# Pages for weights at sixteen 4-byte places of a 64-byte line, in a seven-product fp32r matmul kernel

## The chip, the cores and the metric

The kernel runs on one NeuronCore of a Trainium2 chip, as one launch. The metric is the device time of that launch in microseconds, lower is better. Times are medians over runs; the profile is one execution taken apart by the hardware profiler.

## The reference

The depth is one, so only the short-convolution layer of the model runs, on 1024 positions of width 1024 with an inner width of 2048. All data is float32.

```python
D_MODEL = 1024; SEQ = 1024; D_INNER = 2048; SC_WIDTH = 3; EPS = 1e-6

def rms_norm(x, g):
    return x * rsqrt(mean(x * x, axis=-1) + EPS) * g

def short_conv_mixer(u, w_in, conv_w, w_out):
    z, bg, cg, v = split(u @ w_in, 4, axis=-1)      # w_in: 1024 x 8192
    y = bg * causal_dwconv(cg * v, conv_w) * silu(z) # 3 taps
    return y @ w_out                                 # w_out: 2048 x 1024

u = rms_norm(x, pre_norm)
out = x + rms_norm(short_conv_mixer(u, w_in, conv_w, w_out), post_norm)
```

## The kernel before

Both matrix products are done by a seven-product scheme (products `a` to `g` in place of eight half-size ones), and three of the seven (`b`, `f`, `g`) are cut by seven once more in most chunks; the pieces of that second level carry a prime (`a'` to `g'`) and the word "deep" in their tiles' names. float32 accuracy comes from splitting each operand into a high and a low part in fp32r, so one product of 128 rows costs three matmuls: low by high, high by low, high by high.

The first product takes the input's columns in 16 chunks of 128, two pairs of blocks a chunk (`p` is the pair). The moving operand of its matmuls is a U tile: the normed, transposed input, or a sum of its quarters, split into high and low. The U tiles of the first level (`u_a` to `u_g`) have a pool of their own (`up`, seven tiles of 16 KB a partition) and are read 512 columns at a time (256 for the deep products that use a half of them); the U tiles of the second level (`ubch_deep` and the like) lie in a later pool (`tmp`) and are read 256 columns at a time. The stationary operand is a block of weights, 128 by 128, out of a *page*.

A page is a tile of 512 fp32 numbers (2048 bytes) in each of 128 partitions, made by `page()`. There are 32 of them (`PAGES`). Raw weights arrive in pages from memory (`fetch`, tiles `raw`), GpSimd and VectorE form their sums in pages (`add_s`, `deep_sums`: `se`, `sc`, `sf`, `dsb`, ...), ScalarE rounds a page to its high part and VectorE subtracts that from the source to give the low part (`split`, `split_low`, `split_by_bank`: `wah` and `wal`, `dwb0h` and `dwb0l`, ...), again in pages. Snapshots of finished products (`sna`, `snc`, `sne`), y in transit, raw data of the second matrix product and the residual rows are in pages too. In the second matrix product (from about 615 us) both matmul operands lie in `up` tiles.

The whole program is recorded first and then ordered by a planner (`Plan.arrange`), which simulates the five engines with costs and due times, gives each new page a slot number (0 to 31) from a queue of free ones, and writes the order out; the pages of the head get theirs from `HEAD_SLOTS`. Engines then run their queues in that order and wait for each other by semaphores. Slot `n` is a tile with the tag `pg{n}` and one buffer; its place in SBUF follows from the order in which the tags are first asked for. In the program as built the 32 pages stand back to back from byte 117824 of a partition, 2048 bytes apart, so that each begins at a multiple of 64 bytes; the U tiles of `up` do too (bytes 3136, 19520, ...). The U tiles of `tmp` begin 32 bytes past such a multiple (191584, 193632, ...), because `gpad`, which stands ahead of them in the pool, takes 4128 bytes. The tile class below is what hands out the place.

Of the kernel before, what the change touches and what calls it, by code (L numbers as in the profile page):

```python
# [157 lines left out]
        return out  # L158


class Tile(View):

    __slots__ = ("pool", "args", "kw", "made", "parts", "writes", "reads", "left", "space", "key", "read", "summed", "n", "slot")
# [11 lines left out]
    def get(self):  # L175
        if self.made is None:
            kw = self.kw
            if kw["tag"] == "pg":
                kw = dict(kw, tag=f"pg{self.slot}", bufs=1)
            self.made = self.pool.pool.tile(list(self.args[0]), self.args[1], **kw)  # L180
        return self.made


# [1882 lines left out]
```

## Time and profile before

| what | value |
|---|---|
| time, median of 3 runs | 773.36 us (773.21 to 773.51) |
| time of the profiled execution | 772.83 us |
| its span, first to last instruction | 771.0 us |
| granted TensorE clock, mean | 0.998 |
| PE busy | 762.2 us, 4320 matmuls |
| DVE, ACT, POOL busy | 673.9, 458.8, 462.2 us |
| hardware DMA queue of SyncE | 49.0% of 16 DMA engines' span |

The profiled execution is 0.5 us below the median, and its span 1.8 us below its own time. Every compute instruction is recorded under line 252, the helper that plays a recorded operation, so instructions are told apart by their tiles' names. A matmul's duration includes its latency and overlaps that of its neighbours; how fast the matmuls follow each other is read from their starts, or from how long a run of them takes in the chain of waits.

### The profile page before, as it was taken

The page shows a single profiled execution, that of the slowest core. Times are in us where ns is not written, and L with a number is a line of the kernel's source. Part 1 is how long each engine was busy: PE and PEld are TensorE (multiplying, and loading weights), DVE is VectorE, ACT ScalarE, POOL GpSimd, SP SyncE. Part 2 cuts the span into 40 slices and gives each one's busy share as a digit, 9 for nine tenths or more (in the row PEclk, how much of TensorE's full clock was granted, in tenths as well). Part 3 has the DMA queues.
Part 4 walks back from the last instruction along what each step waited for, and adds up shares of the span by engine and source line. Part 5 has one row for each costly group of instructions (what it writes and reads, how often), then busy time and mean ns, then how long its engine had stood idle before and what let it go on. Part 6 is the DMA issues. An engine that isn't in the chain of part 4 may idle for free.

```text
span 771.0 us, 12816 instructions
## 1 busy us (share of the span) xinstructions
PE 762.2 (99%) x4320; PEld 669.6 (87%) x4320; DVE 673.9 (87%) x1022; ACT 458.8 (60%) x880; POOL 462.2 (60%) x416
## 2 busy tenths in 40 slices
PE   8999999999999999999999999999999999999996
PEld 7888889898889898888888898988888889889885
DVE  6899988989988978989999989798999898877993
ACT  7765678575656565556556565556653656564831
POOL 2519997889575778696789777584739100600321
PEclk9999999999999999999999999999999999999999
DMA  9222325243333547576858474927465998666842
GB/s 318 66 56 82 119 85 152 101 126 131 97 116 96 171 111 209 126 191 158 239 137 254 116 215 107 249 84 213 122 180 174 335 367 293 197 218 206 274 150 109
DMA packets 117137, 130.11 MB, mean 169 GB/s; under 512 B 7320, under 2 KB 74704, under 8 KB 116944
## 3 DMA queue, kind: packets, MB, share of 16 engines
q1 hardware_dynamic: 112560, 120.77, 49.0%
q0 software_dynamic: 4352, 8.39, 7.1%
q8 instruction: 34, 0.56, 0.3%
q14 instruction: 31, 0.25, 0.1%
q10 hardware_dynamic: 160, 0.14, 0.0%
HBM read 101.74 MB, written 44.30 MB: 189 GB/s over the span
## 4 chain that ended last, share of the span: by engine, by line
PE 98%; DVE 1%; DMA 0%; ACT 0%; POOL 0%; issue 0%; POOLq 0%; ACTq 0%
PE px L252 39%; PE pv L252 15%; PE po_x L252 11%; PE px2b L252 5%; PE px2f L252 4%; PE px2g L252 3%; PE po_v L252 3%; PE pp L252 3%; PE pv2b L252 3%; PE pv2f L252 2%; PE pf_x L252 1%; PE pb_x L252 1%; PE py2b L252 1%; PE pv2g L252 1%; PE py L252 1%; PE pf_v L252 1%
## 5 line engine op out<-in xcount | busy, mean ns | idle before, releaser
L252 PE MATMUL px<-u_d,wdh 128*128 128x512 f32 x248 | 76.8, 390 | 0.0
L252 PE MATMUL px<-u_a,wah 128*128 128x512 f32 x248 | 76.7, 390 | 0.0
L252 PE MATMUL pv<-u_e,weh 128*128 128x512 f32 x248 | 76.7, 390 | 0.0
L252 PE MATMUL px<-u_c,wch 128*128 128x512 f32 x248 | 76.6, 390 | 0.0
L252 ACT COPY beside<-raw 128x512 f32<-128x512 f32 x67 | 39.6, 591 | 31.8 <-DVE wal L252 11.0
L252 PEld LDWEIGHTS px<-u_d,wdh 128*128 128x128 f32 x248 | 46.6, 188 | 9.1
L252 PEld LDWEIGHTS px<-u_c,wch 128*128 128x128 f32 x248 | 46.7, 188 | 9.0
L252 PEld LDWEIGHTS px<-u_a,wah 128*128 128x128 f32 x248 | 46.7, 188 | 8.9
L252 PEld LDWEIGHTS pv<-u_e,weh 128*128 128x128 f32 x248 | 46.6, 188 | 8.9
L252 DVE SCALAR_TENSOR_TENSOR cv<-gpad,cw,cv 128x1024 f32<-128x1024 f32 x32 | 49.7, 1554 | 3.4 <-ACT cv L252 3.3
L252 POOL TENSOR_TENSOR sf<-raw,sc 128x512 f32<-128x512 f32 x30 | 44.5, 1482 | 10.9 <-DVE sc L252 6.0
L252 PE MATMUL px<-u_d,wdl 128*128 128x512 f32 x124 | 48.7, 393 | 0.0
L252 PE MATMUL px<-u_a,wal 128*128 128x512 f32 x124 | 48.7, 393 | 0.0
L252 PE MATMUL px<-u_c,wcl 128*128 128x512 f32 x124 | 48.5, 392 | 0.0
L252 PE MATMUL pv<-u_e,wel 128*128 128x512 f32 x124 | 48.5, 391 | 0.0
L252 POOL TENSOR_TENSOR sc<-se,raw 128x512 f32<-128x512 f32 x25 | 36.5, 1460 | 19.0 <-DVE se L252 10.0
L252 ACT COPY sna<-px 128x512 f32<-128x512 f32 x30 | 17.6, 586 | 49.4 <-PE px L252 47.7
L252 POOL TENSOR_TENSOR raw<-raw,raw 128x512 f32<-128x512 f32 x31 | 44.8, 1446 | 3.3 <-DVE se L252 1.9
L252 POOL TENSOR_TENSOR rs_post<-ve_post,minus_half 128x1 f32<-128x1 f32 x7 | 5.4, 784 | 68.1 <-DVE ve_post L252 68.1
L252 POOL TENSOR_TENSOR se<-raw,raw 128x512 f32<-128x512 f32 x22 | 33.1, 1504 | 17.7 <-DMA raw<-in_sc_w_in 5.7
L252 DVE TENSOR_TENSOR wcl<-sc,wch 128x512 fp32r<-128x512 f32 x31 | 31.6, 1020 | 2.6 <-ACT wch L252 2.6
L252 DVE TENSOR_TENSOR sna<-px2b,sna 128x256 f32<-128x256 f32 x56 | 23.2, 413 | 11.9 <-PE px2b L252 11.9
(486 smaller groups left out, 2637.1 us busy)
## 6 DMA issues: line engine op xcount, KB each, us to landing
raw<-in_sc_w_in SPq DMA_DIRECT2D x128, 256.0 KB, 4.6
y_d<-cv SPq DMA_DIRECT2D x16, 512.0 KB, 3.1
s_d<-s SPq DMA_DIRECT2D x32, 256.0 KB, 4.8
t_d<-in_sc_w_out POOLq DMA_DIRECT2D x16, 512.0 KB, 8.2
tb<-in_sc_w_out SPq DMA_DIRECT2D x16, 256.0 KB, 3.0
t_d<-in_sc_w_out SPq DMA_DIRECT2D x16, 256.0 KB, 4.5
t_d<-t_d SPq DMA_DIRECT2D x16, 256.0 KB, 4.5
s<-y_d SPq DMA_DIRECT2D x16, 256.0 KB, 4.7
```

The source lines that it names most:

```text
L252: getattr(engine, name)(*(self.plain(a) for a in args), **{k: self.plain(a) for k, a in kw.items()})
```

## The change

A page of a slot below 28 (`SHIFTED`) is made 8 numbers (32 bytes) longer, and the kernel uses 512 of its 520 numbers, beginning `slot // 2 % 8` numbers in. As the pages stand back to back in descending slots for the most part, their beginnings alternate between a multiple of 64 bytes and 32 past it, and the added 0 to 28 bytes give sixteen places, 4 bytes apart. Slots 28 to 31 stay as they were, and so does a shifted slot whose place comes out at 0. Everything that uses a page (DMA, the three vector engines, the weight loads) finds it at its new place. The U tiles of `up` stay at their bytes; those of `tmp` move up by 896 bytes as a whole and still begin 32 past a multiple of 64. Apart from line numbers, each engine's queue has the same instructions in the same order, on the same tiles and slots.

In the program as built, 3402 matmuls take their weights from a page. Counted by the distance in bytes, modulo 64, between the beginning of the moving operand and that of the weights:

| distance | matmuls before | matmuls after |
|---|---|---|
| 0 | 2700 | 622 |
| 32 | 702 | 280 |
| any of the other fourteen | 0 | 2500 |

Of the 3402, 2710 have their weights at a place other than a multiple of 64 bytes after the change, and none has before.

```diff
+SHIFTED = 28
+
+
 class Tile(View):
...
             kw = self.kw
             if kw["tag"] == "pg":
                 kw = dict(kw, tag=f"pg{self.slot}", bufs=1)
-            self.made = self.pool.pool.tile(list(self.args[0]), self.args[1], **kw)
+            shape = list(self.args[0])
+            whole = int(np.prod(shape[1:]))
+            at, more = 0, 0
+            if kw["tag"][:2] == "pg" and self.slot < SHIFTED:
+                at, more = self.slot // 2 % 8, 8
+            if more:
+                t = self.pool.pool.tile([shape[0], whole + more], self.args[1], **kw)[:, at : at + whole]
+                names = "abcd"[: len(shape) - 1]
+                sizes = dict(zip(names[1:], shape[2:]))
+                self.made = t.rearrange(f"p ({' '.join(names)}) -> p {' '.join(names)}", **sizes)
+            else:
+                self.made = self.pool.pool.tile(shape, self.args[1], **kw)
         return self.made
```

## The prediction

> **What bounds the kernel now.** I read the page first, then the waits of PE, then the chain of waits, stage by stage.
>
> ```profile
> span 771.0 us, 12816 instructions
> PE   8999999999999999999999999999999999999996
> PE 98%; DVE 1%; DMA 0%; ACT 0%; POOL 0%; issue 0%; POOLq 0%; ACTq 0%
> ```
>
> PE is busy in every slice, and the chain that ended last is PE for 98% of the span. The waits of PE (engine, what waited, for whom; us in total, times, longest) are these three, and asked from 60 us on, the same view has none:
>
> ```profile
> PE pw L252 <- DVE idle L252: 1.1, 1, 1.1
> PE pp L252 <- ACT u_a L252: 0.5, 1, 0.5
> PE pk L252 <- DVE xa L252: 0.3, 1, 0.3
> ```
>
> So the time is the sum of the spacings between matmuls. Only two things can move it: the spacing, or a wait that is not there now. The spacing stands in the chain of waits (start us, us, what), first in the second matrix product, where nothing alternates:
>
> ```profile
> 615.09 21.76 PE po_x L252 x96
> 636.85 2.87 PE pb_x L252 x24
> 639.73 2.88 PE pb_y L252 x24
> ```
>
> 96 matmuls of 512 columns take 21.76 us, 226.7 ns each; 24 of 256 columns take 2.88 us, 120.0 ns. Twice 120.0 less 226.7 is 13.3 ns: each matmul pays about 13.3 ns beside its columns (106.7 ns for 256), whatever their number. Times some 4200 matmuls that is 56 us, so a few ns of it are worth a few us. Now a stretch of the first product, and the weight loads of its three kinds of matmul:
>
> ```profile
> 385.89 0.70 PE px2b L252 x6
> 386.59 0.70 PE pv L252 x6
> 387.29 0.72 PE px L252 x6
> ```
>
> ```profile
> L252 PEld LDWEIGHTS px2b<-ubgh_deep,dwb 128*128 128x128 f32 x56 | 9.5, 188 | 0.5
> L252 PEld LDWEIGHTS py2b<-u_b,dwb0h 128*128 128x128 f32 x56 | 8.7, 192 | 0.0
> ```
>
> All eighteen are 256 columns by weights from a page. The first twelve read their moving operand from `ubg*_deep` and `ufg*_deep`, 32 bytes past a multiple of 64, and take 1.40 us, 116.7 ns each; the last six read `u_g`, at a multiple of 64 like the weights, and take 120.0 ns. The loads beside them last 188 ns in the first kind and 192 in the second. This is the one thing in the profile that goes with the place in a line: with weights and moving operand 32 bytes apart a matmul costs 3.3 ns less, and its load 4 ns less, than with both at the same place. When the two are read is in the timeline (start us, us):
>
> ```profile
> 419.42 0.28 PE L252 MATMUL px2f<-ufdh_deep,dwf2h 128*128 128x256 f32 x1
> 419.43 0.19 PEld L252 LDWEIGHTS px2f<-ufdh_deep,dwf2l 128*128 128x128 f32 x1
> ```
>
> The next load starts 0.01 us after a matmul does, so both begin to read at nearly the same moment. Two streams that start together at the same place of a line and meet there would explain both rows.
>
> **The change part by part.** *Spacing.* No instruction is added, removed or moved; what changes is the distance between the streams. The program has 2700 matmuls at distance 0 now and 622 after, so 2078 more are apart. If apart saves 3.3 ns wherever the two places lie (the row shows 32 bytes alone), that is 2078 x 3.3 ns = 6.9 us less. If the saving grows with the distance up to 32 bytes and falls again, the sixteen places give a part: counting each matmul of the built program by its distance (0 to 8 steps of 4 bytes, 0.41 ns a step) gives a total of 12174 steps after against 5616 before, 2.7 us less. If it grows over the whole line, to 15 steps, 7.8 us. Since a collision of two streams is there or not, I take 6.9. That a 512-column matmul saves as much is not shown; its fixed 13.3 ns being the same is why I assume it.
>
> *VectorE.* Its operands from two pages now differ in place. Neighbouring rows: the taps of the convolution read `gpad` 4 or 8 bytes past a line's beginning and `cv` 32 past it; the last row has both sources at multiples of 64.
>
> ```profile
> L252 DVE SCALAR_TENSOR_TENSOR cv<-gpad,cw,cv x32: 1268/1334/2317, 67.8 to 612.0; 128x1024 f32<-128x1024 f32 x32
> L252 DVE SCALAR_TENSOR_TENSOR u_e<-xb 128x1024 fp32r<-128x1024 f32 x2 | 2.4, 1214 | 0.0
> L252 DVE TENSOR_TENSOR gpad<-px,sna x15: 674/691/693, 83.4 to 606.4; 128x512 f32<-128x512 f32 x15
> L252 DVE TENSOR_TENSOR sne<-px,sne x31: 674/677/692, 53.6 to 609.0; 128x512 f32<-128x512 f32 x31
> ```
>
> The shortest tap (min/median/max ns) is 1268 against 1214 ns, 54 more in 1024 columns, 27 for a page. The other pair writes at 8 bytes past a line and at a line, both from 674 ns: writing off the line costs nothing. So 0 to 27 ns for an instruction with both sources in pages. In the stage with the weights (stretch; then busy us and instructions of each engine)
>
> ```profile
> 60.00:615.00 555.00, 555.00 (x3219) 490.84 (x3218) 496.97 (x739) 334.09 (x645) 411.58 (x367) 1.00 0.54 154
> ```
>
> VectorE has 739 instructions and is busy 496.97 of 555 us. At 27 ns for every one it would be 20 us more, 517 of 555: still under PE, but it delivers some low parts late:
>
> ```profile
> 419.01 0.68 DVE L252 TENSOR_TENSOR wdl<-beside,wdh 128x512 fp32r<-128x512 f32 x1
> 419.78 0.19 PEld L252 LDWEIGHTS px<-u_d,wdl 128*128 128x128 f32 x1
> ```
>
> Here `wdl` is done at 419.69 and loaded at 419.78, with 0.09 us to spare; of 587 first uses of split tiles in the trace, seven have under 0.52 us. Ten instructions in a row at 27 ns are 0.27 us late, so these few cost at most 0.3 us each, 2 us in all; and since PE itself would come sooner, the margins shrink further. I take 1.5 us, between 0 and 3. ScalarE (334 us) and GpSimd (412 us) are further from PE; the same 4% on them is hidden behind PE's 555.
>
> *DMA.* Pages are written and read by DMA off the line.
>
> ```profile
> raw<-in_sc_w_in SPq DMA_DIRECT2D x128, 256.0 KB, 4.6
> ```
>
> A raw block lands 4.6 us after its issue. No row shows a load to such a place; bounds are 0 and, at twice the time, 4.6 us later. The planner asks for pages up to 24 us ahead (`ahead`, `sync`), and no wait of PE names a DMA, so I take nothing; without that cover a late block stops GpSimd's sums, then PE.
>
> *Sum.* 772.83 (profiled) - 6.9 + 1.5 = 767.4; from the median of 773.36 it is **768.0 us**.
>
> **The rivals.** *Slower: weights off the line load longer, and the load is in the path.* For it: the 13.3 ns that do not depend on the columns look like a load that PE cannot hide. A block's 512 bytes a partition are eight lines of 64, 1.67 ns each if the 13.3 ns are their reading. Off the line they touch nine: 1.67 ns x 2710 matmuls = 4.5 us more; read as four parts of 128 bytes, each part touches three lines in place of two, half as much again, 6.7 ns x 2710 = 18 us. Against it: the deep moving operands start off a 64-byte line and got no dearer; but 32 is a round place, and 2, 4 or 12 bytes past one are not in the profile. It decides as soon as an off-line load costs more than the 6.9 us gained, 2.5 ns a matmul. At the lower price and without a gain: 773.4 + 4.5 + 1.5 = 779.4 us; at the upper, 792.9. [...]
>
> *No effect on PE: the weights' place does not matter, only the moving operand's.* The 3.3 ns would then belong to where the deep U tiles begin, which stays. For it: in the rows above the two always change together. What is left is VectorE's price: 773.4 + 0 to 1.5, say 774.0 us. [...]
>
> *A smaller gain*, by the rule that grows with the distance: 773.4 - 2.7 + 1.0 = 771.7 us, and VectorE, nearer to its bound, may eat it.
>
> **How the numbers follow.** About 0.2%, 1.5 us, is what a measurement of this kernel can tell from no change. The forecast, PE saving 5 to 9 us: 0.35. The smaller gain: 0.13, of which 0.02 ends within 1.5 us. No effect on PE: 0.18, of which 0.11 within and 0.07 slower by VectorE's late parts. Off-line loads dearer: 0.34, a third of it partly repaid by the gain but slower still. That makes faster 0.46, within 0.13, slower 0.41. Both signs hold much; the forecast's own range is 764 to 771. The whole range reaches down to 759 (the full 7.8 us, no late parts, and as much again for 512-column runs that follow 256-column ones) and up to 784, into the dearer loads, leaving out about 2 in 10, mostly the upper price.
>
> **What would show it.** In the chain of waits after the change, runs of matmuls on `u_g` or `u_b` by pages should take 116 to 118 ns each (0.70 us for six) and those of 512 columns about 223 ns, while `po_x` and `pb_x`, whose operands have not moved, stay at 226.7 and 120.0. The LDWEIGHTS of `py2b<-u_b,dwb0h` should last 188 ns, not 192. If that group or the spacing grows, it is the first rival; if both stay to the ns, the second. A wait of PE for DVE in the stage from 60 to 615 us would be VectorE's price; one for a `raw` DMA would be the cover that I counted on and did not have. The forecast is wrong if the spacing of `u_g` runs stays at 120 or above.

## The result, and the profile after

The changed kernel takes 779.70 us (median of three, 779.45 to 780.08) against 773.36: a ratio of 1.0083, 95% interval 1.0060 to 1.0105. It is 6.3 us slower; forecast was 5.4 us faster. The profiled execution took 780.08 us. The page of the changed kernel begins like that of before, PE being the chain for 98% again:

```profile
span 778.3 us, 12816 instructions
PE   8999999999999999999999999999999999999996
PE 98%; DMA 1%; ACT 0%; DVE 0%; POOL 0%; issue 0%; SPq 0%; POOLq 0%; ACTq 0%
```

Its waits of PE are all in the first stage; asked from 60 us on, the view has none:

```profile
PE pk L266 <- DVE ve_pre L266: 1.3, 1, 1.3
PE pw L266 <- DVE idle L266: 1.1, 1, 1.1
PE pk L266 <- DVE xa L266: 0.7, 1, 0.7
PE pp L266 <- ACT u_a L266: 0.5, 1, 0.5
```

The one wait that before did not have (`ve_pre`, 1.3 us) comes and goes between kernels: 0.3 us in a kernel below that took 779.58 us, none in the one that took 770.25. The stretch of the first 300 matmuls took 1.2 us longer, its waits included, so waits don't explain 6 us. The spacing does. In the stage from 60 to 615 us PE never stops, and the row of that stretch (busy us and instructions of PE, its loads, VectorE, ScalarE, GpSimd) counts what it gets through:

```profile
60.00:615.00 555.00, 555.00 (x3190) 485.58 (x3189) 476.03 (x732) 329.16 (x637) 384.12 (x365) 1.00 0.53 149
```

Before it was 3219 matmuls in the same 555 us, now 3190: 29 fewer at 172 ns is 5.0 us lost in this stage. The granted clock is 1.00 in both. The second product, whose operands have not moved, is unchanged to the hundredth in the chain of waits:

```profile
622.35 21.76 PE po_x L266 x96
644.11 2.87 PE pb_x L266 x24
646.98 2.88 PE pb_y L266 x24
```

Which matmuls got slower is in the groups by form (busy us, mean ns of one). A matmul's duration is longer than the spacing (390 ns for 512 columns that start 228.57 ns apart in the mean, before), so only its change counts. Three groups of before, and the same after:

```profile
L252 PE MATMUL px<-u_d,wdh 128*128 128x512 f32 x248 | 76.8, 390 | 0.0
L252 PE MATMUL px2b<-ubgh_deep,dwb 128*128 128x256 f32 x56 | 12.1, 279 | 0.0
L252 PE MATMUL pv2b<-u_b,dwb1h 128*128 128x256 f32 x56 | 10.7, 283 | 0.0
```

```profile
L266 PE MATMUL px<-u_d,wdh 128*128 128x512 f32 x248 | 77.7, 394 | 0.0
L266 PE MATMUL px2b<-ubgh_deep,dwb 128*128 128x256 f32 x56 | 12.2, 281 | 0.0
L266 PE MATMUL pv2b<-u_b,dwb1h 128*128 128x256 f32 x56 | 10.6, 281 | 0.0
```

512 columns cost 4 ns more, deep ones 2 ns more, and only the third kind, 256 columns from a U tile of the first level, 2 ns less. Averaging the times between neighbouring starts in the two traces (without the first 300 matmuls and without gaps above 300 ns) gives the account; "512 columns" are all matmuls of that size on `u_a` to `u_g`, "deep" those on the U tiles of the second level:

| matmuls by weights in pages | counted | before, ns | after, ns | change |
|---|---|---|---|---|
| 512 columns | 1566 | 228.57 | 232.53 | +6.2 us |
| 256 columns, `u_b`, `u_f`, `u_g` | 936 | 119.37 | 118.53 | -0.8 us |
| 256 columns, deep | 702 | 117.43 | 118.34 | +0.6 us |

Together +6.0 us, and the time from matmul 300 to the last one grew by 6.1. The first 300, which the averages leave out (198 of them are of 512 columns by pages), took 63.0 us in place of 61.8, waits included. That makes up the 7.3 us between the two spans; the medians are 6.3 apart.

The tables below give the same three means for each kernel that was run.

### The profile page after: what moved, and what is told of

Its sections match the earlier page's. It is cut to its first block, busy times and chain, and to the rows that moved or that the text cites. A ratio compares the mean times of both kernels' runs of the same rounds, so it can differ in the third digit from the quotient of the medians.

```text
span 778.3 us, 12816 instructions
## 1 busy us (share of the span) xinstructions
PE 767.9 (99%) x4320; PEld 668.3 (86%) x4320; DVE 656.9 (84%) x1022; ACT 458.1 (59%) x880; POOL 435.3 (56%) x416
## 4 chain that ended last, share of the span: by engine, by line
PE 98%; DMA 1%; ACT 0%; DVE 0%; POOL 0%; issue 0%; SPq 0%; POOLq 0%; ACTq 0%
PE px L266 39%; PE pv L266 15%; PE po_x L266 11%; PE px2b L266 5%; PE px2f L266 4%; PE px2g L266 3%; PE pp L266 3%; PE po_v L266 3%; PE pv2b L266 3%; PE pv2f L266 2%; PE pf_x L266 1%; PE pb_x L266 1%; PE py2b L266 1%; PE py L266 1%; PE pv2g L266 1%; DMA xa<-in_x 1%
## 5 line engine op out<-in xcount | busy, mean ns | idle before, releaser
L266 POOL TENSOR_TENSOR sf<-raw,sc 128x512 f32<-128x512 f32 x30 | 41.7, 1390 | 19.5 <-DVE sc L266 7.9
L266 DVE SCALAR_TENSOR_TENSOR cv<-gpad,cw,cv 128x1024 f32<-128x1024 f32 x32 | 47.8, 1494 | 3.5 <-ACT cv L266 3.2
L266 POOL TENSOR_TENSOR sc<-se,raw 128x512 f32<-128x512 f32 x25 | 33.1, 1322 | 19.0 <-DVE se L266 9.1
L266 POOL TENSOR_TENSOR raw<-raw,raw 128x512 f32<-128x512 f32 x31 | 42.0, 1355 | 2.4 <-DVE se L266 2.1
L266 POOL TENSOR_TENSOR se<-raw,raw 128x512 f32<-128x512 f32 x22 | 29.8, 1357 | 23.1 <-DVE wal L266 5.8
L266 DVE TENSOR_TENSOR wcl<-sc,wch 128x512 fp32r<-128x512 f32 x31 | 29.9, 964 | 3.3 <-ACT wch L266 3.1
```

The costliest lines, as they stand in the source:

```text
L266: getattr(engine, name)(*(self.plain(a) for a in args), **{k: self.plain(a) for k, a in kw.items()})
```

## Experiments: is it uneven places, or the weights' own place?

My theory after the result was the distance between weights and moving operand; its rivals were that neighbouring weights at unequal places are what costs, or pages at a place that is not a multiple of 64 bytes or of some smaller number. Four kernels follow, with 773.15 us for the kernel before beside them. The first moves all pages, and what lies behind them, up by the same 32 bytes:

```diff
+    pad = plan.pool(ctx.enter_context(tc.tile_pool(name="pad", bufs=1)), 1)
+    pad_t = pad.tile([P, 8], F32, tag="pad", name="pad_t")
     pages = plan.pool(ctx.enter_context(tc.tile_pool(name="pages", bufs=PAGES)), PAGES)
...
+    nc.gpsimd.memset(pad_t, 0.0)
```

> All 32 pages begin 32 bytes past a multiple of 64, packed 2048 bytes apart as before (a 32-byte tile stands ahead of them); the U tiles of the first level stay at multiples of 64 and those of the second level move to multiples of 64, so all 3402 matmuls have their operands 32 bytes apart and all weights are at one place. Distance theory (the forecast): spacing of 256 columns 116.7 ns, of 512 about 223.4, about 9 us less on 2700 matmuls, 765 to 768 us. Line theory (the first rival, by 64-byte lines): every weight block is off its line, 1.67 ns or more on 3402 matmuls, 779 us or more. Unequal-neighbours theory (new: the spacing rises where loads that follow each other lie at different places): all places are equal, so 773 us, within 0.3% of before, with 226.7 ns for 512 columns.

The other three are the changed kernel with one line different, in this order: places 0 and 32, places 0 to 48 in steps of 16, and places 4 and 36.

```diff
-                at, more = self.slot // 2 % 8, 8
+                at, more = 0, 8
...
+                at, more = self.slot // 2 % 2 * 4, 8
...
+                at, more = 1, 8
```

> Pages of slots 0 to 27 are 32 bytes longer as in the change, but their use begins at 0: places 0 and 32 alone, mixed, no fine 4-byte offset. Distance theory: about half of the first-level matmuls gain 3.3 ns, 770 us. [...] Unequal-neighbours theory: as slow as the change, 778 to 780 us.

> Places 0, 16, 32 and 48, mixed, all multiples of 16 bytes. [...] Line theory by 64-byte lines: 2086 matmuls off, 777 us. Unequal-neighbours theory: 778 to 780 us, as the change. Distance theory: 768 us.

> Slots 0 to 27 all begin one number in: places 4 and 36 (and 0 for four pages). [...] Unequal-neighbours theory: 778 to 780 us. If fine places cost more than coarse ones, this one is slower than the places 0 and 32 alone by over 2 us; if not, the two agree within 1 us.

| kernel | us | ratio, 95% | 512 | 256 | deep |
|---|---|---|---|---|---|
| all pages up 32 | 779.58 | 1.0081 (1.0064 to 1.0098) | 232.98 | 118.32 | 116.75 |
| places 0, 32 | 778.73 | 1.0072 (1.0057 to 1.0087) | 232.07 | 118.07 | 118.26 |
| places by 16 | 778.27 | 1.0065 (1.0050 to 1.0080) | 231.94 | 118.14 | 118.13 |
| places 4, 36 | 779.32 | 1.0077 (1.0062 to 1.0093) | 232.23 | 118.33 | 118.48 |

All four lose what the change loses, to within 1.3 us. Sixteen different places are not needed: one common shift of 32 bytes does it, so uneven neighbours are not what the loss needs (that they cost nothing of their own is not shown by this, and a later run speaks against it). Nor does the fineness of the place matter beyond about 1 us (779.32 with places 4 and 36, 778.73 and 778.27 with 0 and 32 and by 16). In the changed kernel itself, matmuls of 512 columns whose weights did begin at a multiple of 64 bytes were as slow as the others: 232.7 ns in the mean of 360, against 232.5.

The next two leave the pages at multiples of 64. One moves only the U tiles off it (pad of 32 bytes ahead of `up` and another ahead of the pages: U at 32, pages at 0 modulo 64); the other moves both by 32 (one pad, ahead of `up`), so that the distance is what it was.

```diff
+    pud = plan.pool(ctx.enter_context(tc.tile_pool(name="pud", bufs=1)), 1)
+    pud_t = pud.tile([P, 8], F32, tag="pud", name="pud_t")
     up = plan.pool(ctx.enter_context(tc.tile_pool(name="up", bufs=7)), 7)
```

> Pages back at multiples of 64 bytes; all seven U tiles of the first pool begin 32 past one (second-level U tiles too, as before). All weights of the first product are on their line, all operands 32 bytes apart; the second product has both operands at 32. Theory of the weights' own place (any block off a 64-byte line costs, line theory): nothing is off in the first product, 773 us or, with the 256-column gain, 771. Theory of the distance, as the uniform shift suggests (only a distance of 0 lets runs of 512 columns settle at 226.7 ns; any other gives 232 to 233): 779 us, 512 columns at about 233 and 256 at 117 to 118 in the first product, 226.7 and 120.0 in the second.

> One 32-byte tile ahead of everything: U tiles and pages all begin 32 bytes past a multiple of 64, so the distance is 0 for the first-level matmuls as before, and the second-level U tiles are 32 away. Distance theory: 773 us, as before, 226.7 ns for 512 columns. Theory of the weights' own place: all 3402 blocks off the line, 779 us.

The first took 779.46 us, 1.0080 (1.0065 to 1.0095), with 232.98, 118.33 and 116.74 ns. The second took 773.13 us, 1.0002 (0.9993 to 1.0012), with 228.57, 119.36 and 117.45. The rows of the stretch from 60 to 615 us, of the first and then of the second:

```profile
60.00:615.00 555.00, 555.00 (x3192) 484.68 (x3191) 489.05 (x732) 330.54 (x638) 410.02 (x365) 1.00 0.53 150
```

```profile
60.00:615.00 555.00, 555.00 (x3218) 490.84 (x3218) 499.37 (x739) 334.46 (x645) 410.58 (x367) 1.00 0.54 154
```

3192 matmuls as after, 3218 as before. No page begins off a multiple of 64 in the first, and all do in the second. So the loss goes with the distance between the two operands, not with where the weights lie.

## Experiments: distance modulo what?

A measuring kernel of back-to-back runs on one U tile, weights from pages in 4-byte steps:

> The spacing by itself: no norm, convolution or result, zeros are stored; 42 runs of 96 matmuls (low by high, high by low, high by high, four blocks in turn, as in the kernel) on one moving operand, one after the other on PE with nothing waited for. fiv_a to fiv_p: 512 columns, weights 0, 4, ... 60 bytes past a line, moving operand at 0; tfs_a to tfs_p the same with 256 columns; then both at 32 (yi), both at 4 (xb), moving at 32 or 4 with weights at 0 (ya, xa), and low and high parts of the weights at different places (mix). Distance theory: fiv_a, fiv_yi and fiv_xb at 226.7 ns, every other fiv at 231 to 234; tfs_a, tfs_yi, tfs_xb at 120.0, every other tfs at 116 to 119. Theory of the weights' own place: fiv_ya and fiv_xa at 226.7, fiv_yi and fiv_xb above. [...]

Its high and low tiles were allotted 64 bytes apart modulo 256, which I had taken for the same place. The chain of waits has (start us, us for 96 matmuls):

```profile
30.49 22.39 PE fiv_a L111 x96
...
365.55 22.08 PE fiv_p L111 x96
```

`fiv_a`, with everything at a multiple of 64, takes 233.2 ns a matmul; no run of 512 columns came below 230.0. So 64 is not the step. The built program has `fiv_a` at distances of 64, 128 and 192 bytes modulo 256. The second measuring kernel keeps high and low at the same distance and goes through 0 to 496 bytes in steps of 16:

> A measuring kernel, not the computation: runs of 60 matmuls, each with its own weight load, on one U tile, with weights from pages whose distance from the moving operand goes through 0 to 496 bytes in steps of 16 (512 columns, then 256), and then six runs in which low and high parts lie at different distances. Theory A (a matmul of 512 columns settles at 226.7 ns only where the distance is a whole multiple of some number of bytes, at 230 to 235 elsewhere): distance 0 gives 226.7; if the number is 64, so do 64, 128, 192 and so on; if 128, then 128, 256, 384; if 256, then 256 alone; if 512 or more, none else. 256 columns: 120.0 at those distances and 115 to 119 elsewhere. Theory B (the time does not hang on the distance but on the length of a page's stride or on something else in the program): all 32 distances agree within 1 ns.

The chain of waits, runs of 60: 512 columns at 0, 16, 32 and 192 bytes (`xa`, `xb`, `xc`, `xm`) and at 256, 272 and 288 (`ya`, `yb`, `yc`), then 256 columns at 0, 64, 224 and 320, and last 512 columns with the low parts of the weights at 0 and the high parts at 64 (`mix_xa_xe`):

```profile
26.23 13.60 PE fiv_xa L140 x60
39.83 13.61 PE fiv_xb L140 x60
53.43 13.99 PE fiv_xc L140 x60
...
193.18 13.73 PE fiv_xm L140 x60
...
248.53 13.60 PE fiv_ya L140 x60
262.13 13.61 PE fiv_yb L140 x60
275.74 13.99 PE fiv_yc L140 x60
...
470.84 7.19 PE tfs_xa L140 x60
...
499.30 6.81 PE tfs_xe L140 x60
...
570.03 7.00 PE tfs_xo L140 x60
...
612.68 6.81 PE tfs_ye L140 x60
...
697.61 14.00 PE mix_xa_xe L140 x60
```

The second half of each series repeats the first to 0.01 us: the distance counts modulo 256. For 512 columns (13.60 us is 226.7 ns, 13.99 us is 233.2) 0, 16 and 240 bytes give 226.7 once settled; the other thirteen give 228.9 to 234.3. For 256 columns it is the other way round: 120.0 ns settled at 0 (7.19 us), and less at most others, down to 113.5 at 64 (6.81 us). So what the change saves on short matmuls it loses, several times over, on long ones. The 116.7 ns that the prediction read off the deep matmuls belong here too: their weights stood 224 bytes ahead modulo 256 (from 191584 to 117824), and `tfs_xo` at 224 takes 7.00 us for 60, 116.7 each.

The last row shows that a matmul's neighbours count as well: a third of its matmuls, low weights by the high moving part, stand at distance 0, and still all 60 take 14.00 us, 233.3 ns each, where a third at 226.7 and the rest at 233.2 (the spacing at 64 bytes as at 32) would give 231.0. The kernels with mixed places agree. Taking the places from the built programs, their 512-column matmuls at distance 0 modulo 256 took 231.7 ns (248 of them, places 0 and 32), 231.4 (180, by 16) and 231.4 (48, the changed kernel), against 228.57 before. So uneven neighbours do cost something where places are mixed; the loss does not need them, as the uniform shift shows.

Now back in the kernel. Two uniform shifts of the pages by 64 and 256 bytes (the pad above with 16 and 64 numbers), and one kernel that moves the deep U tiles alone, by making `gpad` ahead of them 160 bytes longer (773.32 us for the kernel before):

> All pages and what lies behind them moved up by 64 bytes, U tiles where they were: distance 64 for 1764 matmuls of 512 columns and 936 of 256, 32 as before for the 702 deep ones. Theory A (what counts is the distance of weights and moving operand modulo 256, with the spacings of the measuring kernel: 233.3 ns for 512 columns and 113.3 for 256 at 64): 1764 x (233.0 - 228.6) = +7.8 us and 936 x (113.3 - 119.4) = -5.7 us, so 775.3 us, with runs of u_b and u_g on pages at 113.3 ns. Theory B (any distance other than 0 is the same, as a shift of 32 seemed to say): 256 columns at 118.3, 512 at 233.0, so 779.5 us as with 32.

> The same with 256 bytes in place of 64. Theory A: modulo 256 nothing has changed, so 773.2 us within 0.5, 512 columns at 228.6 ns in the mean and 256 at 119.4. Rival (the step is 512 or more bytes, and the measuring kernel's equal values at 0 and 256 are its own): 232 to 233 ns and 779 us.

> Pages and U tiles of the first level where they were; the deep U tiles alone moved up by 160 bytes, so that their 702 matmuls have their weights 64 bytes ahead modulo 256 in place of 32 behind. Theory A: 702 x (113.3 - 117.4) = -2.9 us, so 770.3 us, with runs on ubg_deep and the like at 113.3 ns (0.68 us for six). Theory B (64 is one distance among others): 116 to 119 ns, 772.5 to 774 us.

| kernel | us | ratio, 95% | 512 | 256 | deep |
|---|---|---|---|---|---|
| all pages up 64 | 776.75 | 1.0050 (1.0036 to 1.0064) | 233.00 | 114.44 | 117.60 |
| all pages up 256 | 773.37 | 1.0002 (0.9993 to 1.0011) | 228.57 | 119.37 | 117.43 |
| deep U tiles at 64 | 772.18 | 0.9985 (0.9976 to 0.9995) | 228.18 | 119.13 | 117.21 |

256 bytes are no distance at all: 773.37 us against 773.32, with 228.57 ns for 512 columns as before. With 64 the chain of waits shows the gain on `u_b` and `u_f` (`pv2b`, `pv2f`) and the loss on `u_d` (`px`, x12) side by side; the row behind it is that of the same `px` in before:

```profile
383.00 0.69 PE pv2b L252 x6
383.68 0.68 PE pv2f L252 x6
384.36 0.70 PE px2b L252 x6
385.07 0.70 PE px2f L252 x6
385.76 2.79 PE px L252 x12
```

```profile
383.14 2.75 PE px L252 x12
```

Six in 0.68 us are 113.3 ns, as measured alone; twelve in 2.79 are 232.5. The time of 776.75 is 1.4 above what I expected: the 936 matmuls of 256 columns came to 114.44 ns in the mean, not 113.3, which is 1.1 us of it. The third kernel is faster by 1.1 us, and its interval just leaves out no change, but its deep matmuls stayed at 117.2 ns where I had expected 113.3; 0.6 of the 1.1 us are in the 512-column matmuls (1566 at 0.39 ns), whose distance did not change.

## A version that is faster than both

`u_b`, `u_f` and `u_g` are read 256 columns at a time in 936 of 1164 matmuls; the other U tiles of the first level are read 512 at a time only. So these three, the deep U tiles and five tiles of the second product are put 64 bytes below their weights modulo 256, and everything else stays at distance 0. Slots of `up` become tiles of their own, some with spare room ahead:

```diff
+EXTRA = {"b": 48, "c": 16, "f": 48, "g": 16}
+NEAR = set("u_g u_f u_b oB2_b oB3_b ox_b oB1_f oB2_f".split())
...
+            if kw["tag"] == "u":
+                s = SLOT_OF[kw["name"]]
+                kw = dict(kw, tag=f"u{s}", bufs=1)
+                more = EXTRA.get(s, 0)
+                at = more if (kw["name"] in NEAR) == (s in "bf") else 0
+            if kw["tag"] == "gpad":
+                more = 40
```

> A version meant to be faster than both: whatever is mostly read 256 columns at a time as moving operand (u_b, u_f, u_g, the deep U tiles, and in the second product oB2_b, oB3_b, ox_b, oB1_f, oB2_f) begins 64 bytes below the place of its weights modulo 256; everything else stays at distance 0. Theory A: 936 x (113.3 - 119.4) = -5.7, 702 x (113.3 - 117.4) = -2.9, 192 x (113.3 - 120.0) = -1.3, and 228 matmuls of 512 columns on u_b, u_f and u_g pay 4.7 ns = +1.1, in all -8.8 us, 764.4 us. Theory B (distance 64 no better than 32): -1.0 + 0.5 + 1.1 = about 774 us. A third way (PE comes sooner and finds its weights not ready): waits of PE for DVE or POOL between 60 and 615 us, and a time between 765 and 772 us.

It took 770.25 us, 0.9959 (0.9947 to 0.9972): 3.1 us faster than before and 9.4 faster than the changed kernel, with no wait of PE after 60 us. But the terms came out otherwise than expected: 227.41, 117.75 and 117.80 ns. The chain of waits of the same products as above:

```profile
380.54 0.71 PE px2b L282 x6
381.25 0.71 PE px2f L282 x6
381.96 2.72 PE px L282 x12
384.68 0.71 PE px2b L282 x6
385.38 0.71 PE pv L282 x6
386.09 0.71 PE px L282 x6
```

At 64 bytes six matmuls take 0.71 us here, 117.8 ns by their starts, not 0.68. On the other hand the 512-column run behind them takes 2.72 us, 226.7 ns from its first matmul on; before, such a run began with five or six of 228 to 236 ns and took 2.75. That is where 1.8 us come from (1566 at 1.16 ns; the 138 of them on the moved tiles, at 233.3 ns, are in that mean); the 256-column ones of `u_b`, `u_f`, `u_g` give 1.5, those of the second product 0.9 (336 from 119.96 to 117.15 ns). The deep ones take back 0.3 (702 at 0.37 ns), and the first 300 matmuls, 90 of them of 512 columns on moved tiles, 0.7: 62.5 us in place of 61.8. That leaves 3.2, the difference between the two spans.

## Experiments: one distance, two spacings

So 256 columns at 64 bytes run at 113.3 ns in one kernel and at 117.8 in another. Two theories: the run before decides (history), or the moving operand's own place does. One more kernel brings `u_b`, `u_f`, `u_g` to 16 bytes, where 512 columns had been at 226.7 when measured alone, and two measuring kernels switch between distances, on two U tiles at different places. The first of these measuring kernels had its pages 128 bytes further away than its names say, so its "0" is 128, its "64" is 192 and its "192" is 64.

> A measuring kernel, not the computation: runs of 24 matmuls (48 at first), on two U tiles whose beginnings stand at 128 and at 0 modulo 256, in the order 512 columns at distance 0, 256 at 64, 512 at 0, 256 at 0, 512 at 0, 256 at 0, 256 at 64, 512 at 0, then 256 at 16, at 240, 512 at 16, 256 at 16, 224, 192, 208 with 512 at 0 between. Theory H (history: at one distance there are two settled spacings, and the run before decides): 256 at 64 takes 117.7 ns right after a settled run of 512 and 113.3 after a run of 256 at 0, alike on both U tiles; and 512 at 0 starts at 226.7 at once after the first of these, and only after three or more matmuls of 230 to 236 ns after the second. Theory P (place: with the moving operand at 0 modulo 256 distance 64 costs 117.7, with it at 64 or 128 it costs 113.3): each U tile has one value, whatever ran before.

> As b2_near64, with u_b, u_f and u_g 16 bytes below the place of the weights in place of 64 (the deep U tiles stay 64 below; in the second product oB3_b, ox_b, oB1_f, oB2_f 64 below). Theory A (512 columns settle at 226.7 at a distance of 16 as at 0): the 228 matmuls of 512 columns on these three go from 232 to 233 ns back to 226.7, -1.3 us, and 936 of 256 columns go from 117.75 to 118.3, +0.5, so 769.4 us if the 512-column runs behind them still begin at 226.7; if they have to settle again as they did before (mean 228.6), +1.8 us, 771.2. Theory B (in this kernel any distance but a multiple of 256 is dear for 512 columns): 228 of them stay at 232, 770.7 us or above.

> The runs of m3_history with the distances that were meant there: its pages stood 128 bytes further from the U tiles than their names say, so its 512 at 0 was 512 at 128. Here 512 columns at 0 really are at 0, on a U tile at 128 (names in z) and on one at 0 (names in o), modulo 256. Theory H (the run before decides which of two settled spacings a distance takes): 256 at 64 takes 117.7 ns right after settled 512 columns (zb, ob) and 113.3 after 256 at 0 (zg, og); the 512 columns at 0 behind begin at 226.7 at once in zc, oc and with three or more of 230 to 236 in zh, oh; 512 at 16 (zm, om) stays at 226.7 right after settled 512 at 0 and may settle elsewhere (zo, oo) after 256 columns. Theory P (the moving operand's own place decides): z and o differ, and zb equals zg.

The chain of waits of the first, 256 columns at 64 bytes (`zr`, and `or` on the other U tile), and then of the second with 512 at 0, 256 at 64, 512 at 0, 256 at 0, 256 at 64 again (`zg`), and the second U tile (`ob`):

```profile
104.98 2.73 PE zr_256at L112 x24
...
199.06 2.73 PE or_256at L112 x24
```

```profile
27.64 10.88 PE za_512at L112 x48
38.52 2.83 PE zb_256at L112 x24
41.35 5.47 PE zc_512at L112 x24
...
55.16 1.43 PE zf_256at L112 x12
56.59 2.83 PE zg_256at L112 x24
...
130.92 2.83 PE ob_256at L112 x24
```

Place is out: the two U tiles, at 0 and 128 modulo 256, agree to 0.3 ns in every pair of runs that came behind the same run (2.73 us for 24 in `zr` and `or`, 2.83 in `zb` and `ob`). That one distance has two settled spacings is shown, on the same page and the same U tile: 256 columns at 64 bytes take 2.73 us for 24 (113.7 ns) after 512 columns at 128 bytes, and 2.83 us (117.9) after 512 at 0. But history in the form that I had written down fell: after 256 at 0 it is 2.83 as well, where I expected 113.3. Which start leads to which spacing is open. It also limits the list of 0 to 496 bytes above: both of its halves go through the distances in one order, so its values are those of that order.

The kernel with 16 bytes took 771.54 us, 0.9976 (0.9966 to 0.9987), with 229.05, 117.71 and 116.94 ns. In it the deep tiles at 64 bytes showed both spacings on the same tiles: `px2f` after `u_f` at 16 bytes took 0.68 us for six in the chain of waits,

```profile
380.57 0.70 PE pv2f L283 x6
381.27 0.69 PE px2b L283 x6
381.96 0.68 PE px2f L283 x6
```

and behind a settled 512-column run 117 to 119 ns each by their starts. The 138 matmuls of 512 columns at 16 bytes that the averages hold stood at 233.6 ns, though the measuring kernels had that distance at 226.7 to 227.0 each time: in this kernel 16 bytes were not free for 512 columns, as the second theory had it, and its time (770.7 us or above) fits too. The time also lies near the first theory's worse case (771.2 us), and the 512-column runs at distance 0 did have to settle again (228.6 ns in the mean), but the ground that this theory stood on did not hold.

## Why the prediction was wrong

**What bounds the kernel** held: the time went with the spacing of PE, and no wait came in after 60 us.

**The step that failed** is the one that carried the 256-column saving over to 512 columns: "That a 512-column matmul saves as much is not shown; its fixed 13.3 ns being the same is why I assume it." Measured, 512 columns paid 4.0 ns more each in the mean, where the sum had 3.3 less for each that was taken apart, and they are about two thirds of the matmuls that stood at distance 0 (1764 of 2700). Where the sum had a collision of two streams that every distance but 0 relieves, the runs showed a spacing that hangs on the distance modulo 256 with opposite signs for the two sizes: 226.7 ns at 0 against 233.2 at 32 bytes for 512 columns. Equal fixed parts at one distance said nothing of how they change with it. The rows of before could not have shown the opposite sign, as no 512-column matmul in them was at another distance; the range should then have held both signs for this term by itself, and did so only through a rival with another mechanism. The sign named for being wrong, runs on `u_g` at 120 ns or above, did not come (118.5 in the mean of the three tiles): it watched the short matmuls and not the size for which the saving was assumed.

**The term that was right in kind** was mis-sized: 256 columns by pages saved 0.84 ns in the mean, where the sum had 3.3 for each that was taken apart. I had counted distances modulo 64; they count modulo 256, and the saving runs from 0 to 6.5 ns over them (120.0 to 113.5). The deep matmuls, which I took to be apart already, lost 0.9 ns each. The load of `py2b` by `dwb0h` did go from 192 to 189 ns, nearly the 188 forecast. The second row is a load for 512 columns after the change; the last is the same load before:

```profile
L266 PEld LDWEIGHTS py2b<-u_b,dwb0h 128*128 128x128 f32 x56 | 8.6, 189 | 0.0
L266 PEld LDWEIGHTS px<-u_d,wdh 128*128 128x128 f32 x248 | 46.6, 188 | 9.7
```

```profile
L252 PEld LDWEIGHTS px<-u_d,wdh 128*128 128x128 f32 x248 | 46.6, 188 | 9.1
```

The load for 512 columns stayed at 188 ns while the spacing of 512 columns grew by 4.0. In these rows a load's length is no sign of the spacing.

**VectorE**, +1.5 us in the sum, was not there: 476.03 us busy for 732 instructions in the stage from 60 to 615 us, 650 ns each, against 672 before. Nor did any late low part make PE wait. **DMA** at nothing was right: a `raw` block landed 4.3 us after its issue, 4.6 before, and no wait of PE names one.

**The rivals.** Slower, at 779.4 us, met the time within 0.3 us by a mechanism that these runs don't have: with weights off a multiple of 64 bytes the loads lasted no longer (188 ns before and after in the rows above). With no page off a multiple of 64 the kernel took 779.46, and with all of them off it 773.13. The 1.67 ns for a line was an estimate from the 13.3 ns; no run shows such a price, nor a line of 64 bytes: the spacings hung on the distance modulo 256. The places 4 and 36 took 1.05 us more than those by 16, but their distances differ as well, so no run here shows what a finer place costs by itself. No effect on PE fell at once: 512 columns went from 228.57 to 232.53 ns in the mean.

What stays open is the mechanism below: why 512 columns run shortest at the same place modulo 256 (226.7 ns) and 256 columns at another (113.5 ns at 64 bytes), and what picks one of two spacings.

## What to carry to other kernels

Here, where every matmul comes with its own weight load, the place of weights and moving operand modulo 256 bytes was worth some per cent, with opposite signs for 512 columns (226.7 ns at distance 0, up to 234.3 elsewhere) and 256 (120.0 at 0, down to 113.5); in another kernel, measure it for each shape that it has, and place the tiles by the shape that reads them most. Don't carry a saving from one size to another when no row shows the second size, and if you must, give that term both signs in the range. When PE never waits, the number of matmuls in a fixed stretch of the trace (3219 against 3190) tells a change of spacing at a glance.

## What the runs showed of the hardware

- In these kernels the spacing of fp32r matmuls that each load their weights hung on the distance between the two operands' places modulo 256 bytes. In one run through the multiples of 16, 512 columns took 226.7 ns at 0, 16 and 240 and 228.9 to 234.3 elsewhere, 256 columns 120.0 at 0 and 113.5 to 120.0 elsewhere; distances 256 bytes larger repeated all of these values to 0.01 us for 60 matmuls.
- At one distance more than one spacing settled: 256 columns at 64 bytes at 113.5 or 117.8 ns, 512 columns at 16 bytes at 226.7 or 233.6. A 512-column run at distance 0 behind a 256-column one took 224 to 236 ns for its first two to eight matmuls in the last measuring kernel (5.45 to 5.49 us for the 24 of a run, 227.1 to 228.8 in the mean), and 226.7 from the first in the version with 64 bytes; what decides is open.
- VectorE's and GpSimd's instructions got shorter with the pages at sixteen places: in the rows of the stage from 60 to 615 us, 672 to 650 ns and 1121 to 1052 ns in the mean. With the U tiles alone 32 bytes past a multiple of 64 it was 668 and 1123 ns. Over the whole span GpSimd was busy 435.3 us with sixteen places and 451.6 with places 4 and 36, against 461.0 to 464.3 in the kernel before and in the ten other versions of it, whose pages begin at multiples of 16 bytes. One profiled execution each; why is open, and PE, which waits for nothing after 60 us before or after the change, hides it.
